# Streaming encoder layer on one core: value products carried past the ends of attention steps, softmax division moved to the output projection, and a new split of the exponentials' parts over ScalarE, VectorE and GpSimd

## The chip, the cores and the metric

The kernel runs on one core of one Trainium2 chip. The metric is the device time of one execution in microseconds (us); the time of a kernel is the median of its runs. Engine names are those of the profile: PE is TensorE's matmul side and PEld its weight loads, DVE is VectorE, ACT is ScalarE, POOL is GpSimd and SP is SyncE, which issues most DMAs.

## The reference

One layer of a hybrid encoder for two groups of requests: a prompt of 2048 new frames and a sample batch of 8 streams with 16 new frames each and 1024 cached ones. Channels are split: half go through a convolution module, half through attention with 8 heads of 64; both meet in one output projection, and a feed-forward network follows. All data are float32.

```
u, q, k, v, logf = _mixer_inputs(x, ...)          # rmsnorm, modulation, one input projection
# attention, per head, causal, with a cumulative forget bias
s = einsum('bqhd,bkhd->bhqk', q, k) * HEAD_DIM ** -0.5
s = s + (cum_q[..., :, None] - cum_k[..., None, :])
s = where(k_pos <= q_pos, s, NEG_INF)
attn = einsum('bhqk,bkhd->bqhd', softmax(s), v)
# convolution module: causal depthwise conv of width 31, LayerNorm over channels, silu
conv_out = silu(layernorm(conv(u_hist)))
mix = concat([conv_out, attn], -1) @ w_out
x = x + g1 * mix
h = rmsnorm(x) * (1 + sc2) + sh2
x = x + g2 * ((silu(h @ w_gate) * (h @ w_up)) @ w_down)
```

## The kernel before, in words

**Stages.** By the trace: the input projection of the convolution and value channels (0 to 345 us), the q and k projection with its norms (345 to 597), attention (597 to 1200), the output projection (1200 to 1407) and the feed-forward network (1407 to the end, line 1456 for its products). Large products are made of three matmuls in fp32r: an operand is split into a high part (a rounding copy) and a low part (what the copy lost), and high x high, high x low and low x high are summed. `parts_of` (L1158) makes the two parts: the copy on ACT (L1160), the subtraction on the engine that it is given (L1161).

**Prompt attention** runs in 16 steps, `STEPS`: head pair p = 0..3 by block of 512 queries qb = 0..3. A step has 8(qb+1) pieces, one for each tile of 128 keys and head; 320 in all. On the diagonal the pieces narrow from 512 to 384, 256 and 128 columns. For each piece `attend` (L954) issues two score matmuls (L973, L977; on the diagonal a mask, L979) into one of three banks `s`, an exponential on ACT (L981) into `ef` (three buffers), the high part of `e` on ACT (L1160), the low part (L1161) on GpSimd for every third piece and on VectorE otherwise, and, some pieces later, three value products (L964) into the bank `pv` of its head. Rows of `V` filled with ones make the sum of the exponentials in the other half of `pv`. `waiting` holds the pieces whose value products are still owed; it is local to a step, and at the step's end it is emptied. Then the step is normalized: four ACT copies of 64 rows (L998, L999), a logarithm and an exponential for the inverse sum (L1001, L1002), three DVE operations for one Newton step and the product (L1003 to L1005), and a store to `cat_d` (L1006).

**Maxima.** The exponentials need each query's maximum beforehand. `score_maxima` (L913) goes through the same scores transposed, 32 to 41 pieces ahead: one matmul (L934, on the diagonal L936 as well) into one of two banks `mx` and a DVE reduction (L937). At a step's end of its own the maxima are reduced to `Z` (L941), transposed by PE (L948, `pz`) and spread by two DVE products with the mask `bm` (L950) into eight rows of `Q2`, from which the score matmul subtracts them.

**Background.** `background` (L856) is woven in between: the LayerNorm of the convolution (`conv_norm`, L705, with the Newton steps of `newton_rsqrt` at L94 to L96) and the attention of the sample streams (`sample_setup`, `sample_batch`), whose products go into the bank `lane` (L716, L721, L1073, L1107). `last_parts` ends the preparation of the stage before, and `first_weights` loads and splits output weights during the last step.

**What sets the order.** Each engine runs its own list in order. The code is written as generators, and `weave` interleaves a step's parts in proportion to their length; a scheduler then orders each engine's list. `self.after` pins one instruction behind another: the first score of a piece stands behind a maximum 32 or more pieces ahead. K, Q1 and Q2 are loaded on GpSimd's queue (L889, L891, L903, L927); values (L906, `vraw`) and the rest on SP's. `vraw` shares a buffer (`rs`) with the logarithms of the step's end.

**Output projection.** `project_out` (L1178) takes 6 blocks of 360 or 368 columns. For each of 8 channel groups, the four of attention first, it loads `cr` from `cat_d` (L1196), for the convolution's applies silu (L1200), splits it into `ch` and `cl`, and accumulates 24 products into eight banks `acc` (L1144).

## Time and profile before

| | |
|---|---|
| time, median of 3 runs | 2820.78 us (2816.55 to 2822.61) |
| the profiled execution's own time | 2814.3 us |
| its span (first to last instruction) | 2812.5 us |
| mean granted PE clock | 0.98 |
| ACT busy in attention (597 to 1200 us) | 433.8 us |
| POOL busy in attention | 179.3 us |
| hardware DMA queue / software DMA queue | 570.73 MB / 25.42 MB |

How to read it: a group's row gives line, engine, operation, output and inputs, the count, the busy time, the mean duration of one in ns, and after the last bar the engine's idle time just before the group's instructions with what ended it. A row of the waits gives who waited for whom, the sum in us, how many times and the longest. PEclk is the granted clock of PE as a share of full speed. A busy time of PE holds waits that overlap: its instructions are pipelined and their records run into one another. Times of lines come from one profiled execution, which was 6.5 us shorter than the median.

### The profile page before, as it was taken

The numbers are of one execution on the slowest core, as the hardware profiler recorded it, in microseconds if no ns is written. First come the engines' busy times: TensorE is split into PE (matmuls) and PEld (weight loads), VectorE is DVE, ScalarE is ACT, GpSimd is POOL, SyncE is SP. The second block draws the span as 40 slices with busy tenths as digits, with TensorE's granted clock in tenths as the row PEclk, the third lists the DMA queues.
The fourth block names the chain that finished last, engine by engine and source line by source line (L and its number), as shares of the span: only waits on it lengthen the run. The fifth ranks groups of instructions, "written<-read, shape, count | busy, mean of one in ns | idle before, by whom it ended". The sixth has DMA issues, their size and how long they took to land. (4 is left out here: it accounts for less than half of the span.)

```text
span 2812.5 us, 48566 instructions
## 1 busy us (share of the span) xinstructions
PE 2718.6 (97%) x16536; PEld 2515.7 (89%) x16536; DVE 2161.9 (77%) x4235; ACT 1428.7 (51%) x2812; POOL 503.9 (18%) x685
## 2 busy tenths in 40 slices
PE   7999999999989999999999999999999999999999
PEld 6999988866667777698999989999999999999999
DVE  2798898989888787546397989877887778666765
ACT  4443323357776777744354446444554446555552
POOL 3454411243333222214201110000000000000000
PEclk9999999979999999999999999999999999999999
DMA  8753657673334766365576869866786769788883
GB/s 325 249 192 107 191 209 267 182 204 109 101 95 128 203 179 189 130 215 179 181 259 209 294 215 308 268 221 218 233 287 214 226 190 319 244 284 257 271 255 116
DMA packets 389960, 599.24 MB, mean 213 GB/s; under 512 B 47136, under 2 KB 250048, under 8 KB 387664
## 3 DMA queue, kind: packets, MB, share of 16 engines
q1 hardware_dynamic: 375248, 570.73, 62.8%
q0 software_dynamic: 14464, 25.42, 3.9%
q8 instruction: 130, 2.13, 0.3%
q14 instruction: 118, 0.97, 0.1%
HBM read 421.97 MB, written 174.08 MB: 212 GB/s over the span
## 5 line engine op out<-in xcount | busy, mean ns | idle before, releaser
L1456 PE MATMUL z<-rT,rW 128*128 128x360 f32 (+1 forms) x8316 | 1383.3, 328 | 5.5 <-ACT rW L1160 1.4
L1456 PEld LDWEIGHTS z<-rT,rW 128*128 128x128 f32 x8316 | 1378.7, 188 | 8.1 <-ACT rW L1160 2.4
L1160 ACT ACTIVATE rW<-rR 128x512 fp32r<-128x512 f32 x714 | 434.4, 617 | 386.8 <-PE z L1456 272.1
L1161 DVE TENSOR_TENSOR rW<-rR,rW 128x512 fp32r<-128x512 f32 x714 | 479.5, 676 | 154.5 <-ACT rW L1160 151.3
L700 DVE SCALAR_TENSOR_TENSOR cv<-cu,cpar,cv 128x384 f32<-128x384 f32 x580 | 311.6, 614 | 2.8 <-ACT cv L698 2.8
L964 PE MATMUL pv<-e,V 128*128 128x512 f32 (+3 forms) x960 | 268.9, 388 | 14.1 <-DVE e L1161 6.3
L964 PEld LDWEIGHTS pv<-e,V 128*128 128x128 f32 x960 | 167.9, 194 | 71.7 <-DVE e L1161 14.6
L937 DVE TENSOR_REDUCE M<-mx 128x1 f32<-128x512 f32 (+2 forms) x320 | 188.7, 603 | 50.2 <-PE mx L934 31.7
L981 ACT ACTIVATE ef<-s 128x512 f32<-128x512 f32 (+3 forms) x320 | 167.1, 532 | 116.7 <-PE s L979 47.1
L512 PE MATMUL z<-hqx,wqh 128*128 128x384 f32 (+1 forms) x768 | 196.6, 333 | 1.0 <-DVE logf L347 1.0
L1160 ACT ACTIVATE rT<-traw 128x360 fp32r<-128x360 f32 (+1 forms) x315 | 149.1, 501 | 91.7 <-DMA traw<-gt_d 62.9
L1161 DVE TENSOR_TENSOR rT<-traw,rT 128x360 fp32r<-128x360 f32 (+1 forms) x315 | 157.6, 531 | 45.0 <-ACT rT L1160 44.7
L1161 POOL TENSOR_TENSOR e<-ef,e 128x512 fp32r<-128x512 f32 (+3 forms) x106 | 127.2, 1200 | 347.4 <-ACT e L1160 180.7
L1160 ACT ACTIVATE e<-ef 128x512 fp32r<-128x512 f32 (+3 forms) x320 | 175.5, 567 | 4.0
L1161 DVE TENSOR_TENSOR e<-ef,e 128x512 fp32r<-128x512 f32 (+3 forms) x214 | 149.1, 704 | 35.4 <-ACT e L1160 34.4
L512 PEld LDWEIGHTS z<-hqx,wqh 128*128 128x128 f32 x768 | 135.7, 188 | 18.9 <-issue 15.3
L934 PE MATMUL mx<-K,Q 96*128 96x512 f32 (+2 forms) x320 | 134.3, 427 | 17.5 <-DVE M L937 11.3
L1144 PE MATMUL acc<-ch,woh 128*128 128x360 f32 (+1 forms) x384 | 127.4, 333 | 10.0 <-ACT ch L1160 4.6
L1384 DVE TENSOR_TENSOR rR<-rR 128x512 f32<-128x512 f32 (+1 forms) x136 | 93.4, 707 | 50.9 <-DMA rR<-w_down 44.1
L973 PE MATMUL s<-Q,K 128*128 128x512 f32 (+3 forms) x320 | 125.8, 393 | 3.4 <-ACT ef L981 3.4
L1144 PE MATMUL acc<-ch,wol 128*128 128x360 f32 (+1 forms) x384 | 126.9, 331 | 0.0
L512 PE MATMUL z<-hqx,wql 128*128 128x384 f32 (+1 forms) x384 | 126.4, 329 | 0.0
(306 smaller groups left out, 3935.4 us busy)
## 6 DMA issues: line engine op xcount, KB each, us to landing
rR<-sup_d SPq DMA_DIRECT2D x176, 256.0 KB
rR<-w_gate SPq DMA_DIRECT2D x132, 256.0 KB
traw<-gt_d SPq DMA_DIRECT2D x154, 180.0 KB
rR<-w_down SPq DMA_DIRECT2D x104, 256.0 KB
rR<-sdn_d SPq DMA_DIRECT2D x96, 256.0 KB
rR<-w_up SPq DMA_DIRECT2D x88, 256.0 KB
sup_d<-rR SPq DMA_DIRECT2D x88, 256.0 KB
wa<-w_ada SPq DMA_DIRECT2D x16, 1024.0 KB
```

What stands on the lines that cost most here:

```text
L512: nc.tensor.matmul(z[:, :n], w[:, m], x[:, :n], start=(c == 0 and k == 0), stop=(c == CB - 1 and k == 2))
L700: self.pin(nc.vector.scalar_tensor_tensor(dst, src, w, acc[i], ALU.mult, ALU.add))
L934: self.mx.append(nc.tensor.matmul(mx[:, :w], Q2[0:AUX, h, j * P:(j + 1) * P], K2[kb][0:AUX, h, :w], start=True, stop=not diag))
L937: nc.vector.tensor_reduce(M[:, i, kb:kb + 1], mx[:, :w], AX.X, ALU.max)
L964: nc.tensor.matmul(z[h][:, off:], V[kt // 4][:, v, kt % 4, h:h + 2, :].rearrange("p b c -> p (b c)"), e[:, x, off:], start=(kt == 0 and i ...
L973: first = nc.tensor.matmul(s[:, off:], K1[kb][:, h, sl], Q1[:, h, off:], start=True, stop=False)
L981: self.last_piece = nc.scalar.activation(ef[:, off:], s[:, off:], AF.Exp)
L1144: self.nc.tensor.matmul(z[:, :n], w[:, m], y, start=(first and i == 0 and k == 0), stop=(last and i == len(terms) - 1 and k == 2))
L1160: copy = self.nc.scalar.activation(hi, raw, AF.Copy)
L1161: engine.tensor_tensor(lo, raw, f32(hi), ALU.subtract)
L1384: nc.vector.tensor_tensor(t, x, y, op)
L1456: nc.tensor.matmul(z, W[:, x, m], t[:, y, :w], start=(k == 0 and i == 0), stop=(k == n - 1 and i == 2))
```

## The change

**Value products.** The list `waiting` belongs to the kernel and is emptied only behind the last step; a piece's value products follow five pieces behind its scores, those of another step among them. The first product of a piece is pinned behind the last score issued (`last_s`). A head's bank is taken when its first value product comes, and its end (`end_of_step`) comes with its last.

**End of a step and division.** `end_of_step` copies the head's whole bank to `zc` on ACT in one operation and stores the row of sums to `sum_d` and the undivided head to `cat_d`. `inverses`, woven into the next step (and behind the last one at once), loads the sums of both heads as 128 x 8, takes the reciprocal on DVE and stores it to `inv_d`. `project_out` loads two broadcast rows of `inv_d` for each attention operand and multiplies on DVE (24 multiplies, 48 loads).

**Parts of the exponentials.** For every second pair of pieces the high part is made by a copy on VectorE, for the others on ACT: 160 and 160. The low part of the first head goes to VectorE and of the second to GpSimd: 160 and 160, where before 214 and 106.

**Maxima.** One DVE copy of 8 rows and eight DMAs of one row each (128 columns) replace the products with `bm`; all maxima go into one row of `Q2`. The lead grows from 32 to at most 43 pieces.

**Queues.** K, Q1 and Q2 are loaded on SP's queue; `vraw` has a buffer of its own.

**Smaller edits.** One Newton step in place of two in the q/k norm and in `conv_norm`; `sample_setup` is cut by yields, and keys and biases of the sample streams are loaded a chunk or a stream ahead (`next_keys`, `next_bias`); background products are pinned behind the last score (`behind`); `xo` has 18 buffers in place of 20.

```diff
-            newton_rsqrt(nc, y, zp.tile([P, NB], F32, tag="t", name="rt", bufs=1)[:, :n], v, 2, self.pin)
+            newton_rsqrt(nc, y, zp.tile([P, NB], F32, tag="t", name="rt", bufs=1)[:, :n], v, 1, self.pin)
...
+            else:
+                parts.append((self.inverses(*STEPS[n - 1]), 4))
...
         drain(back)
+        drain(self.inverses(*STEPS[-1]))
...
-            nc.gpsimd.dma_start(K2[0:HD + 2], rows[HD:])
+            nc.sync.dma_start(f32(K2[0:HD + 2]), rows[HD:])
...
-        raw = self.awk.tile([P, 4, P], F32, tag="rs", name="vraw", bufs=1)
+        raw = self.awk.tile([P, 4, P], F32, tag="vr", name="vraw", bufs=1)
...
-        for h in range(2):
-            nc.vector.tensor_tensor(Q2[r, h, :].rearrange("r (j q) -> r j q", j=4),
-                                    pz[r, :].unsqueeze(1).broadcast_to([8, 4, P]),
-                                    self.bm[r, h, :].unsqueeze(2).broadcast_to([8, 4, P]), ALU.mult)
+        m = self.lp.tile([P, P], F32R, tag="mrow", name="mrow", bufs=1)
+        nc.vector.tensor_copy(m[r], pz[r])
+        for i in range(8):
+            nc.sync.dma_start(f32(Q2[AUX:AUX + 1, i // 4, i % 4 * P:(i % 4 + 1) * P]), f32(m[AUX + i:AUX + i + 1]))
...
         def value(kt, h, off, e):
+            if kt == 0:
+                z.append(self.bank("tr", "pv"))
...
+                if i == 0:
+                    self.after(product, self.last_s)
+            if kt == nkt - 1:
+                self.end_of_step(p, qb, h, z[h])
...
-                self.split3 = (self.split3 + 1) % 3
-                self.parts_of(e[:, 0, off:], e[:, 1, off:], ef[:, off:], nc.gpsimd if self.split3 == 0 else nc.vector)
-                waiting.append((kt, h, off, e))
-                if h and len(waiting) > len(self.eslots) - 3:
-                    value(*waiting.pop(0))
-                    value(*waiting.pop(0))
+                self.turn ^= h
+                if (h ^ self.turn) == 0:
+                    nc.vector.tensor_copy(e[:, 0, off:], ef[:, off:])
+                else:
+                    nc.scalar.activation(e[:, 0, off:], ef[:, off:], AF.Copy)
+                (nc.gpsimd if h else nc.vector).tensor_tensor(e[:, 1, off:], ef[:, off:], f32(e[:, 0, off:]), ALU.subtract)
+                self.waiting.append((value, kt, h, off, e))
+                while len(self.waiting) > min(len(self.eslots) - 2, 5):
+                    self.next_value()
                 yield
-        for w in waiting:
-            value(*w)
-
-        pvs, sm = (wk.tile([P, 512], F32, tag=k, name=k, bufs=1) for k in ("pvs", "sm"))
...
+        if n + 1 == len(STEPS):
+            while self.waiting:
+                self.next_value()
...
+    def end_of_step(self, p, qb, h, z):
+        if h == 0:
+            self.zc = self.awk.tile([P, 2, 512], F32, tag="zc", name="zc", bufs=1)
+        t = slice(qb * 512, qb * 512 + 512)
+        self.last_exp = self.nc.scalar.copy(self.zc[:, h], z)
+        o, x = slice(HD * h, HD * h + HD), HD - HD * h
+        self.nc.sync.dma_start(self.sum_d[2 * p + h:2 * p + h + 1, t], self.zc[x:x + 1, h])
+        self.last_store = self.nc.sync.dma_start(self.cat_d[o, 4 + p, t], self.zc[o, h])
...
+    def inverses(self, p, qb):
...
+        nc.sync.dma_start(r, self.sum_d[2 * p:2 * p + 2, t].rearrange("h (a c) -> a h c", c=4))
+        yield
+        nc.vector.reciprocal(r, r)
+        nc.sync.dma_start(self.inv_d[2 * p:2 * p + 2, t].rearrange("h (a c) -> a h c", c=4), r)
...
+                else:
+                    inv = cp.tile([P, NW], F32, tag="ci", name="ci", bufs=2)[:, :n]
+                    for h in range(2):
+                        load = nc.sync.dma_start(inv[HD * h:HD * h + HD], self.inv_d[2 * (c - 4) + h:2 * (c - 4) + h + 1, b0:b1].broadcast_to([HD, n]))
...
+                    nc.vector.tensor_tensor(raw, raw, inv, ALU.mult)
```

**What the order shows: the end of a step on PE.** PE's list of before at the end of the second step (`pv` are the step's value products, `s` scores, `mx` maxima, `lane` background):

```order
L973 MATMUL s_7578<-Q1_7147,K11_6652 128x128 [waits PE_49]
L977 MATMUL s_7578<-Q21_6650,K21_6648 128x128
L979 MATMUL s_7578<-masks_4132 128x128
L964 MATMUL pv_7360<-e_7554,V1_7012 128x256 [waits Activation_49]
L964 MATMUL pv_7360<-e_7554,V1_7012 128x256 [waits DVE_49]
L964 MATMUL pv_7360<-e_7554,V1_7012 128x256
L964 MATMUL pv_7359<-e_7572,V1_7012 128x128 [waits Activation_49]
L934 MATMUL mx_7408<-K23_6658,Q23_6667 128x384 [waits DVE_49]
L936 MATMUL mx_7408<-masks_4132 128x128
L716 MATMUL lane_7630<-cq_7671,ones_112 32x512 [waits Activation_49]
L964 MATMUL pv_7360<-e_7584,V1_7012 128x128 [waits Activation_49]
L716 MATMUL lane_7630<-cq_7674,ones_112 32x512 [waits Activation_49]
```
The rest of the value products stands in the next rows, and then the first score of the third step. PE's list of the changed kernel at the same place; there the score line is L984, the second score L988, the mask L990, the value product L971 and the maximum L939:

```order
L984 MATMUL s_7583<-Q1_7144,K11_6637 128x128 [waits Activation_49]
L988 MATMUL s_7583<-Q21_6635,K21_6633 128x128
L990 MATMUL s_7583<-masks_4134 128x128
L971 MATMUL pv_7401<-e_7542,V1_7013 128x256
L971 MATMUL pv_7401<-e_7542,V1_7013 128x256 [waits DVE_49]
L971 MATMUL pv_7401<-e_7542,V1_7013 128x256
L939 MATMUL mx_7421<-K20_6628,Q23_6652 128x512 [waits DVE_49]
L984 MATMUL s_7599<-Q1_7438,K10_6632 128x512 [waits DMAHW6_49,Activation_49]
L988 MATMUL s_7599<-Q22_6638,K20_6628 128x512 [waits DMAHW4_49,DMAHW5_49,DMAHW3_49,DMAHW2_49]
L971 MATMUL pv_7417<-e_7557,V1_7013 128x256
L971 MATMUL pv_7417<-e_7557,V1_7013 128x256 [waits Pool_49]
```
What moved: the third step's first score stands right behind the second step's last piece, and the value products still owed, three behind each score, follow it.

**The seam on SP.** SP's list of before where attention hands over to the output projection (`cr` are its operands, `raw` its weights, `pvs` the last step's result):

```order
L1323 DMA sp2_13363<-ident 128x128 [waits DVE_49,PE_49]
L1196 DMA cr_13385<-cat_d_71 128x368
L1196 DMA cr_13415<-cat_d_71 128x368
L1196 DMA cr_13445<-cat_d_71 128x368
L1196 DMA cr_13475<-cat_d_71 128x368
L1169 DMA raw_13507<-w_out 128x512 [waits PE_49]
L1169 DMA raw_13511<-w_out 128x512 [waits DMAHW3_49]
L1196 DMA cr_13515<-cat_d_71 128x368 [waits DMAHW6_49,DMAHW4_49,DVE_49]
L1169 DMA raw_13548<-w_out 128x512 [waits DMAHW5_49]
L1006 DMA cat_d_71<-pvs_13325 128x512 [waits DVE_49]
```
And of the changed kernel at the same place (L1023 and L1024 are the stores of `end_of_step`, L1033 and L1036 the load and the store of `inverses`, L1263 the operand, L1271 the inverses for it):

```order
L1023 DMA sum_d_80<-zc_13388 1x512 [waits Activation_49]
L1024 DMA cat_d_71<-zc_13388 64x512
L1023 DMA sum_d_80<-zc_13388 1x512 [waits Activation_49]
L1024 DMA cat_d_71<-zc_13388 64x512
L832 DMA cat_d_71<-catS_8605 128x128 [waits DMAHW5_49,DVE_49]
L1033 DMA inv_13398<-sum_d_80 128x2x4 [waits DMAHW6_49,DMAHW3_49,DMAHW1_49]
L832 DMA cat_d_71<-catS_8605 128x128 [waits DMAHW7_49]
L832 DMA cat_d_71<-catS_8605 128x128 [waits DMAHW0_49]
L832 DMA cat_d_71<-catS_8605 128x128
L1036 DMA inv_d_81<-inv_13398 128x2x4 [waits DMAHW2_49,DVE_49]
L1263 DMA cr_13449<-cat_d_71 128x368
L1271 DMA ci_13453<-inv_d_81 64x368 [waits DMAHW4_49,PE_49]
```
What moved: the operand loads, ahead of the last step's store before, now stand behind the last step's sums, inverses and their waits.

**A stretch of DVE** inside attention. Before (L937 reduces a maximum, L1161 makes a low part, L1003 to L1005 end a step, L950 spreads maxima):

```order
L937 TENSOR_REDUCE M_1_6670<-mx_12246 128x1 [waits PE_49]
L1161 TENSOR_TENSOR e_12360<-ef_12358,e_12360 128x512 [waits Activation_49]
L950 TENSOR_TENSOR Q22_6653<-pz_12250,bm_6633 8x512 [waits PE_49]
L950 TENSOR_TENSOR Q22_6653<-pz_12250,bm_6633 8x512
L937 TENSOR_REDUCE M_1_6670<-mx_12263 128x1 [waits PE_49]
L1083 RECIPROCAL rsx_10310<-rsx_10310 128x1 [waits Activation_49]
L1161 TENSOR_TENSOR e_12371<-ef_12369,e_12371 128x512 [waits Activation_49,Pool_49]
L937 TENSOR_REDUCE M_1_6670<-mx_12283 128x1 [waits PE_49]
L937 TENSOR_REDUCE M_1_6670<-mx_12295 128x1 [waits PE_49]
L1003 TENSOR_TENSOR sm_12330<-sm_12330,rs_12335 128x512 [waits Activation_49]
L937 TENSOR_REDUCE M_1_6670<-mx_12313 128x1 [waits PE_49]
L1004 SCALAR_TENSOR_TENSOR sm_12330<-sm_12330,rs_12335 128x512 [waits DVE_49]
```
And in the changed kernel (L942 reduces a maximum, L999 is the copy of a high part, L1002 the low part, L1228 splits values):

```order
L942 TENSOR_REDUCE M_0_6654<-mx_11920 128x1 [waits PE_49]
L1002 TENSOR_TENSOR e_12011<-ef_12009,e_12011 128x512 [waits Activation_49]
L1228 TENSOR_TENSOR V0_7012<-vraw_11877,V0_7012 128x4x2x64 [waits Activation_49]
L942 TENSOR_REDUCE M_0_6654<-mx_11951 128x1 [waits PE_49]
L942 TENSOR_REDUCE M_0_6654<-mx_11971 128x1 [waits PE_49]
L999 CAST e_12044<-ef_12042 128x512 [waits Activation_49]
L999 CAST e_12058<-ef_12056 128x512 [waits Activation_49,Pool_49]
L1002 TENSOR_TENSOR e_12044<-ef_12042,e_12044 128x512 [waits DVE_49]
L942 TENSOR_REDUCE M_0_6654<-mx_11985 128x1 [waits PE_49]
L942 TENSOR_REDUCE M_0_6654<-mx_12003 128x1 [waits PE_49]
L1002 TENSOR_TENSOR e_12072<-ef_12070,e_12072 128x512 [waits Activation_49]
```
What moved: the operations that end a step are gone, and of four pieces two high parts and two low parts stand on DVE.

More of the change, by code (lines that the diff above doesn't have):

```diff
@@ L715, in channel_mean @@
             for j in range(4):
-                nc.tensor.matmul(pm[32 * j:32 * j + 32, :n], self.ones[:, 0:32], src[j], start=True, stop=True,
+                self.behind(nc.tensor.matmul)(pm[32 * j:32 * j + 32, :n], self.ones[:, 0:32], src[j], start=True, stop=True,
                                  tile_position=(0, 32 * j))
@@ L782, in attention @@
         self.R.close()
-        self.split3 = 0
+        self.split3, self.turn, self.waiting, self.last_s = 0, 0, [], None
         self.Wout = {}
@@ L875, in background @@
         self.smc = self.after_attention.enter_context(self.pool(name="smc", bufs=2))
-        self.sample_setup(bank)
-        yield
+        yield from self.sample_setup(bank)
         for b in range(NS):
@@ L888, in keys @@
             rows = self.k_d[2 * p:2 * p + 2, :, t].rearrange("h r t -> r h t")
-            nc.gpsimd.dma_start(K2[0:HD + 2], rows[HD:])
+            nc.sync.dma_start(f32(K2[0:HD + 2]), rows[HD:])
             k1 = self.K1[(4 * p + kb) % 6]
-            nc.gpsimd.dma_start(k1, rows[0:P])
+            nc.sync.dma_start(f32(k1), rows[0:P])
             K1.append(k1)
@@ L926, in score_maxima @@
             t = slice(qb * 512, qb * 512 + 512)
-            nc.gpsimd.dma_start(Q2[0:HD], self.q_d[2 * p:2 * p + 2, 0:HD, t].rearrange("h r t -> r h t"))
+            nc.sync.dma_start(f32(Q2[0:HD]), self.q_d[2 * p:2 * p + 2, 0:HD, t].rearrange("h r t -> r h t"))
             for i in range(8):
@@ L957, in attend @@
         Q1, Q2 = self.Q1.pop(n), self.Q2[n % 4]
-        z = [self.bank("tr", "pv") for _ in range(2)]
         nkt = 4 * qb + 4
-        waiting = []
+        z = []
         def value(kt, h, off, e):
+            if kt == 0:
+                z.append(self.bank("tr", "pv"))
             for i, (v, x) in enumerate(((0, 0), (0, 1), (1, 0))):
-                nc.tensor.matmul(z[h][:, off:], V[kt // 4][:, v, kt % 4, h:h + 2, :].rearrange("p b c -> p (b c)"), e[:, x, off:],
-                                 start=(kt == 0 and i == 0), stop=(kt == nkt - 1 and i == 2))
+                product = nc.tensor.matmul(z[h][:, off:], V[kt // 4][:, v, kt % 4, h:h + 2, :].rearrange("p b c -> p (b c)"), e[:, x, off:],
+                                           start=(kt == 0 and i == 0), stop=(kt == nkt - 1 and i == 2))
+                if i == 0:
+                    self.after(product, self.last_s)
+            if kt == nkt - 1:
+                self.end_of_step(p, qb, h, z[h])
         for kt in range(nkt):
@@ L995, in attend @@
-        pvs, sm = (wk.tile([P, 512], F32, tag=k, name=k, bufs=1) for k in ("pvs", "sm"))
-        for h in range(2):
-            o, x = slice(HD * h, HD * h + HD), slice(HD - HD * h, P - HD * h)
-            nc.scalar.copy(sm[o], z[h][x])
-            nc.scalar.copy(pvs[o], z[h][o])
-        r = wk.tile([P, 512], F32, tag="rs", name="rs", bufs=1)
-        nc.scalar.activation(r, sm, AF.Ln)
-        self.last_exp = nc.scalar.activation(r, r, AF.Exp, scale=-1.0)
-        nc.vector.tensor_tensor(sm, sm, r, ALU.mult)
@@ L1004, in attend @@
-        nc.vector.scalar_tensor_tensor(sm, sm, 2.0, r, ALU.subtract, ALU.mult)
-        nc.vector.scalar_tensor_tensor(pvs, pvs, -1.0, sm, ALU.mult, ALU.mult)
-        self.last_store = nc.sync.dma_start(self.cat_d[:, 4 + p, qb * 512:(qb + 1) * 512], pvs)
+                self.turn ^= h
[3 more added lines that the diff above has]
+                    nc.scalar.activation(e[:, 0, off:], ef[:, off:], AF.Copy)
@@ L1008, in sample_setup, with behind, issue @@
+    def behind(self, op):
+        def issue(*args, **kw):
+            ins = op(*args, **kw)
+            self.after(ins, self.last_s)
+            return ins
+        return issue
     def sample_setup(self, bank):
@@ L1018, in sample_setup @@
         nc.gpsimd.memset(self.Qbd, 0.0)
+        self.kc, self.S = [], []
+        self.next_keys(0)
+        yield
+        yield
         for h in range(2):
@@ L1029, in sample_setup @@
         for kt in range(8):
-            nc.tensor.matmul(pt[:n, 2 * kt:2 * kt + 2], lf[:, kt, :], self.ones[:, 0:2], start=True, stop=True)
+            self.behind(nc.tensor.matmul)(pt[:n, 2 * kt:2 * kt + 2], lf[:, kt, :], self.ones[:, 0:2], start=True, stop=True)
         suf = sm.tile([P, 8], F32, name="suf")
@@ L1037, in sample_setup @@
             for i in range(4):
-                nc.tensor.matmul(pb[:n, i, :], lf[:, 4 * b + i, :], tri, start=True, stop=True)
+                self.behind(nc.tensor.matmul)(pb[:n, i, :], lf[:, 4 * b + i, :], tri, start=True, stop=True)
             nc.vector.tensor_tensor(
@@ L1072, in sample_batch @@
             for g in range(NP):
-                nc.tensor.matmul(pc[32 * g:32 * g + 32, :w], self.Qbd[:, g, b].rearrange("p h q -> p (h q)"), kt[:, g, :],
-                                 start=True, stop=True, tile_position=(0, 32 * g))
+                self.behind(nc.tensor.matmul)(pc[32 * g:32 * g + 32, :w], self.Qbd[:, g, b].rearrange("p h q -> p (h q)"), kt[:, g, :],
+                                              start=True, stop=True, tile_position=(0, 32 * g))
+            if c < 2:
+                self.next_keys(2 * b + c + 2)
+            else:
+                self.next_bias(b + 1)
             nc.vector.tensor_tensor(S[:, c0:c0 + w], S[:, c0:c0 + w], pc[:, :w], ALU.add)
@@ L1632, in host_layout @@
                             for w in range(2)], 1))
-    bm = np.zeros((P, 2, 4), np.float32)
-    for h in range(2):
-        for j in range(4):
-            bm[AUX + 4 * h + j, h, j] = 1
-    r["bm"] = bm
     r["sel"] = np.concatenate([
```

77 lines of the change are left out of this document (54 added, 23 removed).

## The prediction

> **What bounds the kernel now.** I read the page first (busy shares, then its costliest groups):
>
> ```profile
> span 2812.5 us, 48566 instructions
> ...
> PE 2718.6 (97%) x16536; PEld 2515.7 (89%) x16536; DVE 2161.9 (77%) x4235; ACT 1428.7 (51%) x2812; POOL 503.9 (18%) x685
> ...
> L1456 PE MATMUL z<-rT,rW 128*128 128x360 f32 (+1 forms) x8316 | 1383.3, 328 | 5.5 <-ACT rW L1160 1.4
> ```
>
> PE is the bound, but 97% is a mean over stages. The windows by stage come next (columns: us, then busy us of each engine with its instructions, granted clock, DMA share, GB/s):
>
> ```profile
> core 0: us, PE busy (x) PEld busy (x) DVE busy (x) ACT busy (x) POOL busy (x), PEclk, DMA share, GB/s
> ...
> 345.00:597.00 252.00, 250.69 (x1493) 210.31 (x1491) 233.13 (x573) 85.19 (x178) 59.60 (x101) 1.00 0.70 223
> ...
> 597.00:625.00 28.00, 23.30 (x52) 12.28 (x52) 23.75 (x46) 10.19 (x28) 10.30 (x12) 0.55 0.72 196
> 597.00:1200.00 603.00, 557.53 (x3177) 409.76 (x3176) 477.71 (x828) 433.80 (x879) 179.30 (x176) 0.95 0.51 145
> 1200.00:1407.00 207.00, 198.38 (x1183) 195.91 (x1184) 95.27 (x185) 83.34 (x160) 56.13 (x55) 0.99 0.59 193
> 1407.00:2812.00 1405.00, 1390.57 (x8383) 1386.76 (x8381) 1103.75 (x2139) 687.01 (x1342) 43.68 (x36) 0.99 0.76 244
> ```
>
> The feed-forward stage (1407 to 2812) and the q/k projection (345 to 597) have PE full; the change hardly touches them. Attention, 597 to 1200, holds the loss: 45.5 us of idle PE, and a granted clock of 0.95 that costs another 30 us (5% of 603). A busy PE also hides waits, since records overlap. The feed-forward stage gives the pace: 1405/8316 = 0.169 us for a product of 360 columns, 0.47 ns a column. Attention has 224 pieces of 512 columns and 32 each of 384, 256 and 128: 139,264 columns, in six products each (two scores, three values, one maximum), and some 250 masks of 128 columns: 868,000 columns, 407 us. Background products add about 65 (the largest two lines are below). So PE needs about 472 of 603 us; 30 go to the clock and about 100 to waits. Groups and waits of this window say on whom:
>
> ```profile
> L964 PE MATMUL pv<-e,V 128*128 128x512 f32 x672 | 210.4, 419 | 9.4 <-DVE e L1161 5.2 <-ACT e L1160 2.2 <-POOL e L1161 1.7
> ...
> L937 DVE TENSOR_REDUCE M<-mx 128x1 f32<-128x512 f32 x221 | 149.2, 684 | 37.4 <-PE mx L934 31.7 <-PE mx L936 4.6
> L1160 ACT ACTIVATE e<-ef 128x512 fp32r<-128x512 f32 x224 | 136.4, 632 | 2.0
> ...
> L1161 DVE TENSOR_TENSOR e<-ef,e 128x512 fp32r<-128x512 f32 x150 | 118.2, 795 | 25.2 <-ACT e L1160 24.7
> ...
> L1161 POOL TENSOR_TENSOR e<-ef,e 128x512 fp32r<-128x512 f32 x74 | 98.7, 1334 | 267.6 <-ACT e L1160 132.2 <-issue 40.3 <-PE pv L964 27.9
> ...
> L1073 PE MATMUL lane<-kc,Qbd 128*32 128x512 f32 x128 | 17.6, 622 | 4.1 <-DVE S L1075 4.1
> ...
> L1107 PE MATMUL lane<-vc,pT 128*32 128x128 f32 x512 | 16.0, 274 | 0.0
> ```
>
> ```profile
> PEld mx L934 <- DVE M L937: 27.1, 39, 1.8
> ...
> PEld pv L964 <- DVE e L1161: 14.6, 25, 1.3
> ```
>
> PE waits in turn for the maxima's reductions, which free its banks, and for the low parts: both on DVE, 79% busy here. Part of the idle time lies at ends of steps, where the value products are drained. The last end, in the timeline:
>
> ```profile
> 1193.90 0.27 PE L979 MATMUL s<-masks 128*128 128x128 f32 x1
> ...
> 1195.81 0.42 PE L964 MATMUL pv<-e,V 128*128 128x128 f32 x2
> ...
> 1197.03 0.86 PE L964 MATMUL pv<-e,V 128*128 128x128 f32 x3 [0.81 <-ACT e L1160]
> ```
>
> After the last score come the products still owed, then 0.8 us of nothing, then the rest.
>
> **The change part by part.** Changed line numbers are in the order above; durations below are of before.
>
> *Carried value products.* Only the last step drains. At the other 15 ends five scores of the next step now stand ahead of the step's last value products. I take 1.2 us each (the 0.8 shown and the short waits around it), 18 us; between 0.8 and 2, 12 to 30. The lost clock after 625 is about 17 us (30 less 0.45 × 28 = 12.6); half of it follows such gaps by my guess, 7 us.
>
> *High and low parts.* ACT gives up 160 of 320 copies, about 88 us, and is the bound nowhere in attention: nothing by itself. DVE takes 160 copies, 136 full pieces' worth. No copy of this shape from SBUF stands in the trace; the nearest is the subtraction below at 0.68 us alone, so at most 92 us, and I take 75 for a one-input operation. In return 54 of DVE's 214 low parts go to GpSimd, which then has 160 × 1.2 = 192 us in place of 127. What that does to DVE is seen here, DVE first, GpSimd second:
>
> ```profile
> 1019.81 0.68 DVE L1161 TENSOR_TENSOR e<-ef,e 128x512 fp32r<-128x512 f32 x1
> ...
> 1020.75 1.43 DVE L1161 TENSOR_TENSOR e<-ef,e 128x512 fp32r<-128x512 f32 x1
> ```
>
> ```profile
> 1020.09 1.55 POOL L1161 TENSOR_TENSOR e<-ef,e 128x512 fp32r<-128x512 f32 x1 [1.96 <-PE mx L934]
> ```
>
> A subtraction that starts under GpSimd's takes 1.43 us and ends with or after it; the group's mean of 795 against 680 is that.
>
> The Trainium skill ("VectorE: DVE Perf Modes", The perf-mode tier table) lets an fp32 copy in SBUF run at twice the rate of tensor_tensor (1227 against 2293 ns for 2048 elements). By that the copies would take about 0.36 us each, an estimate from its ratio and 49 us in all, and the sum would gain up to 26 us of DVE time over mine; no trace here shows it.
>
> *Ends of steps, spread, Newton.*
>
> ```profile
> L950 DVE TENSOR_TENSOR Q<-pz,bm 8x512 fp32r<-8x512 f32 x32 | 20.9, 692 | 0.7 <-PE pz L948 0.2
> ...
> L998 ACT COPY sm<-pv 64x512 f32<-64x512 f32 x32 | 18.6, 581 | 5.6 <-PE pv L964 4.9
> ...
> L1004 DVE SCALAR_TENSOR_TENSOR sm<-sm,rs 128x512 f32<-128x512 f32 x15 | 12.8, 850 | 0.0
> ...
> L1005 DVE SCALAR_TENSOR_TENSOR pvs<-pvs,sm 128x512 f32<-128x512 f32 x15 | 12.5, 832 | 0.0
> ...
> L1003 DVE TENSOR_TENSOR sm<-sm,rs 128x512 f32<-128x512 f32 x15 | 12.1, 806 | 0.0
> ...
> L94 DVE SCALAR_TENSOR_TENSOR ct<-cr 128x512 f32<-128x512 f32 x8 | 7.1, 886 | 0.0
> ```
>
> DVE loses 37 us of normalization, about 17 of the spread (a copy of 128 columns stays) and about 10 of Newton steps (half of this row and its two sisters). So DVE in attention: 478 − 38 (54 × 0.70) − 37 − 17 − 10 + 75 = 451, and the lock above grows with GpSimd's share from 21% to 33%: half as much again of its present 25 us or so, and the copies may meet it too, +15 to +50. I take 475, within 3 us of before: no gain from DVE's total, but it comes out of the ends of steps, where it stood in one block. I give 4 us for the bank of maxima that waited behind that block (of 27.1) and 3 for the lane's 4.1 (its loads and products now stand further apart). ACT frees a step's bank in one copy a head.
>
> *Queues.* K and Q loads move from GpSimd to SP, behind SP's stores of sums and rows, and 128 row transfers of 512 bytes follow. In before SP stands still for long:
>
> ```profile
> SPq L906 <- DVE sm L1004: 166.2, 12, 30.5
> ```
>
> That wait goes with the value rows' own buffer. The new SP waits are for the copies at ends of steps and for Q2's free buffer; behind them stand the next K loads, which are asked for seven or more pieces (about 12 us) early. I cost it at nothing; uncovered, one late load per step, 1 us × 15.
>
> *The start.* From 597 to 625 DVE is 85% busy and PE at half clock waits for the first maxima; a Newton step less in the q/k norm and direct transfers for the spread: −4 (0 to −8).
>
> *The seam.* Before, operands of the output projection are requested ahead of the last values; the first product follows the last value by 2.6 us:
>
> ```profile
> 1196.63 1.85 SPq L1196 DMA_DIRECT2D cr<-cat_d  x4
> ...
> 1200.49 0.67 PE L1144 MATMUL acc<-ch,woh 128*128 128x368 f32 x1 [2.60 <-ACT ch L1160]
> ```
>
> ```profile
> SPq L1298 <- DMA ht_d<-nx: 8.6, 8, 2.3
> ```
>
> Now they stand on SP behind the last step's inverses: copy 0.6, store of sums, load, reciprocal 0.2, store, load of inverses, then multiply 0.5 and high part 0.5. Four transfers at about 2.3 us with issue (the longest wait for a small one just quoted) make 9.2, the whole 11 to 12: +9 over before (+5 if transfers land in 1.3, +12 with a half-clock window behind the gap). No PE work stands there to cover it.
>
> *Output projection.* 24 multiplies and 48 transfers more; DVE is at 46% there, but each joins a chain that PE waits for at blocks' starts: +2 (0 to +6).
>
> Sum: −18 −7 −4 −3 −4 +9 +2 = −25; the loose pinning of background products and prefetched keys I put at −3 (0 to −10). −28: 2814.3 − 28 = 2786 for the profiled execution. That one is 6.5 us under the median of 2820.8, so the median is forecast at 2793. A difference of 0.2% (5.6 us) is what a measurement here can tell from none.
>
> **The rivals.** *PE at its pace.* If five pieces of lag cover most waits, attention loses 60 rather than 32 of its 130: total −60 − 4 + 9 + 2 = −53, 2768. For it: no drains, and a wait list made of many short waits (39 in 27.1 us). Against: DVE is not relieved.
>
> *VectorE bound through GpSimd.* Four full pieces now ask of DVE two copies (here at their upper 0.68), two low parts, four reductions: 8 × 0.68 = 5.4 us; PE has 24 products, 24 × 512 × 0.47 ns = 5.8. Two GpSimd subtractions of 1.3 us cover 40% of that time; each of four two-buffer operations meeting one for 0.65 us on average adds 1.0: 6.4, more than PE's 5.8. Over 68 such groups that is 41 us, which eats the 32 and leaves +9: with seam, projection and start +16, about 2837. It decides once copies too are held up by GpSimd. For it is this stretch, in which DVE is full and PE a fifth idle; against, before's reductions (from PSUM) keep 684 ns, and they are half of the load:
>
> ```profile
> 780.00:790.00 10.00, 8.00 (x43) 6.35 (x42) 9.91 (x21) 5.68 (x16) 4.05 (x4) 1.00 0.60 132
> ```
>
> The Trainium skill speaks for this rival: by "SBUF — State Buffer" (SBUF: two separate sides) a copy in a 2-port mode takes the shared port pair for the whole instruction just as a two-input operation does. The trace agrees for two inputs (1.43 against 0.68 us); for copies no run here shows it.
>
> *SP's queue.* The seam costs what I say, and inside attention loads queue late behind stores, 15 us of the 32 being lost: −28 + 15 = −13, at the worst about 0 if rows of the maxima also come late; 2808 to 2821.
>
> *It doesn't do what it says*: the order shows carried products and both splits; 2 in 100.
>
> **How the numbers follow.** Forecast 0.48, PE at its pace 0.22, VectorE bound 0.14, SP's queue 0.14, nothing 0.02. Faster: 0.48 + 0.22 + half of SP's = 0.77; same 0.09 (the rest of SP's and nothing); slower 0.14. The range starts at 2755 (PE at its pace with the seam at +5 and 10 more from the background) and ends at 2824, past SP's worst; it leaves out the VectorE case and a little below.
>
> **What would show it.** Right: value products after every score across ends of steps; PE idle in attention down from 45 to about 25 us; DVE's total near 475 in a stage of about 570; first output product 11 to 12 us after the last value. Wrong: low parts of DVE over 900 ns on average and copies over 0.7 (VectorE bound); K or Q2 awaited by PE (SP's queue); the seam under 5 us, or attention under 545 (PE at its pace).

## The result and the profile after

The changed kernel takes 2841.47 us (median of 4 runs, 2839.34 to 2847.12) against 2818.85 for the kernel before beside it: a ratio of 1.0084, 95% interval 1.0066 to 1.0102. It is slower by 0.84%, outside the range and against the sign of the forecast. The profiled execution took 2839.3 us, with a span of 2837.5.

Where the time went is read from the first and last start of three lines, from the views of the score line, the value line and the products of the output projection (count, then ns as least/median/most, then first to last start in us). Before:

```profile
L973 PE MATMUL s<-Q,K x320: 221/395/796, 624.6 to 1193.6; 128*128 128x512 f32 x112, 128*128 128x384 f32 x16, 128*128 128x256 f32 x16, 128*128 128x128 f32 x16
```

```profile
L964 PE MATMUL pv<-e,V x960: 220/393/796, 631.3 to 1197.6; 128*128 128x512 f32 x138, 128*128 128x256 f32 x25, 128*128 128x384 f32 x15, 128*128 128x128 f32 x14
```

```profile
L1144 PE MATMUL acc<-ch,woh x384: 321/329/674, 1200.5 to 1406.7; 128*128 128x360 f32 x128, 128*128 128x368 f32 x64
...
L1144 PE MATMUL acc<-cl,woh x384: 321/327/412, 1204.8 to 1407.0; 128*128 128x360 f32 x128, 128*128 128x368 f32 x64
```

After:

```profile
L984 PE MATMUL s<-Q,K x320: 222/396/735, 619.0 to 1182.1; 128*128 128x512 f32 x112, 128*128 128x384 f32 x16, 128*128 128x256 f32 x16, 128*128 128x128 f32 x16
```

```profile
L971 PE MATMUL pv<-e,V x960: 219/392/735, 624.1 to 1187.3; 128*128 128x512 f32 x139, 128*128 128x256 f32 x20, 128*128 128x384 f32 x17, 128*128 128x128 f32 x16
```

```profile
L1211 PE MATMUL acc<-ch,woh x384: 322/330/673, 1200.8 to 1432.8; 128*128 128x360 f32 x128, 128*128 128x368 f32 x64
...
L1211 PE MATMUL acc<-cl,woh x384: 321/327/502, 1205.1 to 1433.2; 128*128 128x360 f32 x128, 128*128 128x368 f32 x64
```

| us | before | after | difference | forecast |
|---|---|---|---|---|
| up to the first score | 624.6 | 619.0 | −5.6 | −4 |
| attention: first score to last value product | 573.0 | 568.3 | −4.7 | −35 |
| seam: to the first output product | 2.9 | 13.5 | +10.6 | +9 |
| output projection: first to last product | 206.5 | 232.4 | +25.9 | +2 |
| the rest | 1405.5 | 1404.3 | −1.2 | 0 |

The differences sum to the 25.0 us between the spans. Two terms failed: attention, which gave a seventh of its gain, and the output projection. (The −35 joins the terms of drains, clock, bank, lane and background.)

The windows by stage of the changed kernel, for attention and for the fourth block of the output projection (from its first product to the first of the fifth):

```profile
597.00:1200.00 603.00, 548.16 (x3164) 412.70 (x3164) 455.29 (x866) 323.49 (x643) 200.40 (x174) 0.94 0.50 144
```

```profile
1310.70:1365.40 54.70, 40.38 (x210) 37.64 (x209) 28.68 (x58) 18.51 (x36) 16.02 (x15) 0.87 0.65 202
```

and the same block before:

```profile
1304.40:1341.40 37.00, 34.62 (x208) 33.19 (x209) 24.95 (x48) 14.15 (x27) 16.11 (x15) 1.00 0.69 223
```

DVE has less work in attention than before (455 against 478 us), so more work on it is not what ate the gain, and ACT has 110 us less. This one block of the projection takes 17.7 us more, 54.7 against 37.0, with PE idle for 14.3 and the granted clock at 0.87; the second, third and fifth are 2 to 3 us longer each. Waits in attention of the changed kernel:

```profile
PEld mx L939 <- DVE M L942: 45.4, 50, 3.2
...
PE mx L939 <- DVE M L942: 25.8, 22, 3.0
...
DVE inv L1035 <- DMA inv<-sum_d: 20.9, 9, 4.6
```

PE's waits for value products have gone, as meant; those for the maxima's banks rose (PEld 27.1 to 45.4, PE 11.3 to 25.8). And there is a new line: DVE, which works its list in order, stands nine times, 20.9 us in all, until the sums of a step have come back from memory, since `inverses` put a reciprocal into its list. Everything behind it in DVE's list waits, and the reductions that free the maxima's banks are among it. The forecast costed this load only at the seam.

The seam in the timeline, from the copy of the last step to the first output product:

```profile
1187.19 1.07 ACT L1021 COPY zc<-pv 128x512 f32<-128x512 f32 x2 [0.71 <-PE pv L971]
...
1188.59 0.44 SPq L1023 DMA_DIRECT2D sum_d<-zc  x1
...
1190.36 0.39 SPq L1033 DMA_DIRECT2D inv<-sum_d  x1
...
1192.27 0.20 DVE L1035 RECIPROCAL inv<-inv 128x8 f32<-128x8 f32 x1 [4.07 <-DMA inv<-sum_d]
1192.50 0.37 SPq L1036 DMA_DIRECT2D inv_d<-inv  x1
1192.91 0.47 SPq L1263 DMA_DIRECT2D cr<-cat_d  x1
1193.48 1.11 SPq L1271 DMA_DIRECT2D ci<-inv_d  x2
...
1199.66 0.54 DVE L1274 TENSOR_TENSOR cr<-cr,ci 128x368 f32<-128x368 f32 x1 [7.19 <-DMA ci<-inv_d]
...
1200.80 0.67 PE L1211 MATMUL acc<-ch,woh 128*128 128x368 f32 x1 [13.10 <-ACT ch L1227]
```

This is the chain of the prediction, step by step, but not with its prices. From the store of the sums to the reciprocal it took 3.7 us where two transfers of 2.3 were allowed; the last hop, from the store of the inverses to the multiply, took 7.2 where two more were. And most of that hop is the operand's own load, which now is asked for late. The run e1 below has neither the loads of the inverses nor the multiply, and there the operand still takes 5.1 us from its request to the copy on ACT:

```profile
1194.41 1.89 SPq L1263 DMA_DIRECT2D cr<-cat_d  x4
...
1199.53 0.51 ACT L1227 ACTIVATE ch<-cr 128x368 fp32r<-128x368 f32 x1 [8.40 <-DMA cr<-cat_d]
```

Its seam is 11.3 us, so the loads of inverses and the multiply make only 2.2 of the 13.5.

### The profile page after: what moved, and what is told of

Read it like the earlier page. It is cut to its first block, busy times and chain, and to the rows that moved or that the text cites. A ratio compares the mean times of both kernels' runs of the same rounds, so it can differ in the third digit from the quotient of the medians.

```text
span 2837.5 us, 48644 instructions
## 1 busy us (share of the span) xinstructions
PE 2719.1 (96%) x16536; PEld 2525.4 (89%) x16536; DVE 2142.7 (76%) x4284; ACT 1323.1 (47%) x2588; POOL 529.3 (19%) x675
## 5 line engine op out<-in xcount | busy, mean ns | idle before, releaser
L1228 DVE TENSOR_TENSOR rW<-rR,rW 128x512 fp32r<-128x512 f32 x714 | 479.9, 677 | 163.9 <-ACT rW L1227 159.1
L971 PE MATMUL pv<-e,V 128*128 128x512 f32 (+2 forms) x960 | 259.1, 380 | 0.0
L1002 POOL TENSOR_TENSOR e<-ef,e 128x512 fp32r<-128x512 f32 (+3 forms) x160 | 187.9, 1176 | 360.6 <-DVE e L999 151.6
L942 DVE TENSOR_REDUCE M<-mx 128x1 f32<-128x512 f32 (+2 forms) x320 | 190.9, 604 | 51.7 <-PE mx L939 35.6
L971 PEld LDWEIGHTS pv<-e,V 128*128 128x128 f32 x960 | 171.2, 195 | 30.0 <-issue 1.2
L1228 DVE TENSOR_TENSOR rT<-traw,rT 128x360 fp32r<-128x360 f32 (+1 forms) x315 | 158.7, 534 | 31.0 <-ACT rT L1227 30.6
L939 PE MATMUL mx<-K,Q 96*128 96x512 f32 (+2 forms) x320 | 138.0, 438 | 27.4 <-DVE M L942 25.8
L939 PEld LDWEIGHTS mx<-K,Q 96*128 96x128 f32 x320 | 64.2, 201 | 74.7 <-DVE M L942 45.4
L984 PE MATMUL s<-Q,K 128*128 128x512 f32 (+3 forms) x320 | 127.7, 399 | 0.1
L1211 PE MATMUL acc<-cl,woh 128*128 128x360 f32 (+1 forms) x384 | 125.6, 337 | 0.4 <-DVE cl L1228 0.4
```

The source lines that it names most:

```text
L939: self.mx.append(nc.tensor.matmul(mx[:, :w], Q2[0:AUX, h, j * P:(j + 1) * P], K2[kb][0:AUX, h, :w], start=True, stop=not diag))
L942: nc.vector.tensor_reduce(M[:, i, kb:kb + 1], mx[:, :w], AX.X, ALU.max)
L971: product = nc.tensor.matmul(z[h][:, off:], V[kt // 4][:, v, kt % 4, h:h + 2, :].rearrange("p b c -> p (b c)"), e[:, x, off:], start=(kt = ...
L984: first = nc.tensor.matmul(s[:, off:], K1[kb][:, h, sl], Q1[:, h, off:], start=True, stop=False)
L1002: (nc.gpsimd if h else nc.vector).tensor_tensor(e[:, 1, off:], ef[:, off:], f32(e[:, 0, off:]), ALU.subtract)
L1211: self.nc.tensor.matmul(z[:, :n], w[:, m], y, start=(first and i == 0 and k == 0), stop=(last and i == len(terms) - 1 and k == 2))
```

## The experiments

Ratios are to the kernel before on the same chip, with 95% intervals; the stages come from each run's profile as in the table above. Three of these kernels (the changed one, e1, e2) differ by no edit in attention and took 568.3, 568.8 and 574.7 us there: a difference in attention under 6 us between single profiles says nothing, and there the ratios decide. The projection scatters as well: the changed kernel and the five that share its projection (e3, e6, e7, e11, e12) took 232 to 238 us there, three without the division (e1, e8, e10) 215 to 224, those with 20 buffers and the division at the ends of steps 205 to 208. Attention, seam and projection are in us.

| run | ratio (interval) | attention | seam | projection |
|---|---|---|---|---|
| changed | 1.0084 (1.0066 to 1.0102) | 568.3 | 13.5 | 232.4 |
| e1 | 1.0041 (1.0026 to 1.0055) | 568.8 | 11.3 | 218.6 |
| e2 | 1.0031 (1.0018 to 1.0044) | 574.7 | 11.7 | 220.4 |
| e3 | 1.0101 (1.0079 to 1.0122) | 574.6 | 13.3 | 234.7 |
| e4 | 1.0042 (1.0026 to 1.0059) | 575.1 | 2.9 | 218.7 |
| e5 | 0.9950 (0.9929 to 0.9970) | 563.6 | 6.4 | 208.3 |
| e6 | 1.0053 (1.0036 to 1.0071) | 556.9 | 12.7 | 236.1 |
| e7 | 1.0160 (1.0138 to 1.0182) | 593.8 | 12.2 | 236.7 |
| e8 | 0.9934 (0.9909 to 0.9958) | 551.3 | 3.0 | 215.4 |
| e9 | 0.9911 (0.9896 to 0.9927) | 559.8 | 2.9 | 207.0 |
| e10 | 0.9955 (0.9942 to 0.9968) | 556.5 | 2.8 | 223.5 |
| e11 | 1.0037 (1.0023 to 1.0052) | 551.3 | 12.9 | 236.4 |
| e12 | 1.0058 (1.0042 to 1.0074) | 560.4 | 13.2 | 237.9 |
| e13 | 0.9955 (0.9940 to 0.9970) | 564.4 | 4.8 | 207.2 |
| e14 | 1.0003 (0.9991 to 1.0014) | 571.4 | 3.4 | 206.6 |
| e15 | 0.9948 (0.9931 to 0.9965) | 568.7 | 5.0 | 205.4 |
| e16 | 0.9909 (0.9879 to 0.9939) | 557.5 | 4.7 | 205.9 |
| e17 | 0.9875 (0.9843 to 0.9907) | 550.5 | 3.0 | 208.0 |

**The output projection: e1, e2, e4.** In e2 the tile of ones is filled once, ahead of the blocks, by GpSimd.

```diff
-                    inv = cp.tile([P, NW], F32, tag="ci", name="ci", bufs=2)[:, :n]
...
-                    nc.vector.tensor_tensor(raw, raw, inv, ALU.mult)
+                    pass
```

> The changed kernel without the division in the output projection: no loads of the inverses there, no multiply (its attention output stays undivided; all else, the inverses too, is as in the changed kernel). Theory D (the loss of 26 us in the output projection is the division's doing): the projection falls from 232 us back to about 207, the first output product comes about 9 us after the last value instead of 13.5, and the time falls by about 30 us, to some 2811 us. Rival X (the two buffers taken from xo): the projection stays above 225 us and the time above 2830. Rival V (VectorE in attention is the loss): attention is untouched, so the time stays at 2841 within 4 us.

```diff
-                    nc.vector.tensor_tensor(raw, raw, inv, ALU.mult)
+                    nc.vector.tensor_tensor(raw, raw, one[:, :n], ALU.mult)
```

> As the run without the division, but the 24 multiplies stay, by a tile of ones that is already there: the 48 loads of inverses alone are left out (the output stays undivided). If the loads on SP's queue and their landing are what the division costs: as the run without the division, within 4 us. If it is the multiply in VectorE's row: 10 us or more above it, near the changed kernel.

```diff
-                x = sp.tile([P, NW], F32, tag="x", name="xo", bufs=20)
+                x = sp.tile([P, NW], F32, tag="x", name="xo", bufs=18)
```

> The kernel before with 18 buffers for xo in place of 20 and nothing else. Rival X (the buffers): the output projection grows by 10 us or more, 2829 us or above. Theory D: no change from the kernel before, 2819 within 4 us.

Neither theory alone was right; each has half. Without the division the projection falls by 14 us and stays 12 above the kernel before; with 18 buffers in the kernel before it rises by those 12 (206.5 to 218.7). The 24 multiplies without their loads cost nothing that shows (220.4 against 218.6), though DVE stands in front of them for 34.0 us until `cr` lands. So 12 to 14 us come with the 48 loads; whether by their time on SP's queue or by DVE's further wait for them (13.8 us in 7 waits in the changed kernel) was not tried. The buffers act in one block, the fourth, 51.2 us in e4 against 37.0:

```profile
1301.90:1353.10 51.20, 39.64 (x209) 37.77 (x209) 23.75 (x49) 15.30 (x29) 16.01 (x15) 0.86 0.60 196
...
1322.00:1332.00 10.00, 7.47 (x26) 7.24 (x27) 6.05 (x17) 4.27 (x9) 5.42 (x5) 0.50 0.26 90
```

```profile
SPq L1211 <- DMA x_d<-xo: 5.9, 7, 1.7
```

Loads of `xT` wait on SP until a store has freed their buffer (5.9 us, 2.1 with 20 buffers); DVE, which adds a bank's product to `xT` and so frees the bank, waits for them (8.5 us against 3.2), and PE waits for the bank (9.7 against 4.3). For some 10 us of this block the granted clock is 0.50. The buffers' total is shown by e4; the chain, and that the clock falls because PE idles, are read from the trace and have no run of their own.

**The inverses in attention: e3, e8, e10.** e3 put three more yields between the load and the reciprocal.

> The changed kernel with the reciprocal of a step's sums three yields further behind the load that it waits for. Theory R (in attention VectorE stands still for the landing of the sums, 25 us in 10 waits, and the maxima's reductions behind it hold PE): VectorE's wait for the sums falls below 5 us, attention gets 5 to 12 us shorter, 2830 to 2836 us in all. Rival V (VectorE is bound by its work and by GpSimd): the wait goes and the time stays within 3 us of 2841.

It tested nothing: in the order that was run, the reciprocal stands as close behind its load as in the changed kernel, and DVE still waited as long.

```profile
DVE inv L1038 <- DMA inv<-sum_d: 21.6, 9, 5.5
```

e8 leaves the inverses out of the kernel without division, e10 only the reciprocal:

```diff
-                parts.append((self.inverses(*STEPS[n - 1]), 4))
...
-        drain(self.inverses(*STEPS[-1]))
```

> As the run without the division, and without the inverses too: no loads of sums, no reciprocals, no stores of them (the attention output stays undivided). Theory R (VectorE's 21 us of waits for the sums to land cost PE 5 to 12 us in attention): attention falls from some 569 to 562 us or less. Theory M: within 4 us. In both the seam falls from 11 to about 5 us, since no inverse stands ahead of the operands on SP.

```diff
-        nc.vector.reciprocal(r, r)
```

> The run without the division, with the inverses' loads and stores left in and only the reciprocal on VectorE left out (what is stored are the sums; the attention output stays undivided). Theory R (it is VectorE that stands behind the load): attention as without any inverses, 551 us within 4, against 569 with the reciprocal. Theory Q (SP's queue: its waits for the copies and the sums delay what stands behind them): attention near 569 us. The seam, where SP no longer waits for VectorE but still for two landings, falls from 11 to about 7 us in both.

Theory R holds in the main. Without the reciprocal attention falls from 568.8 to 556.5 us (551 within 4 was expected), without all of the inverses to 551.3. By the ratios e10 is 0.86% or 24 us below e1, of which the seam is 8.5. The waits for the maxima's banks fall, from 47.0 and 27.3 us in e1 to these in e10:

```profile
PEld mx L939 <- DVE M L942: 34.3, 41, 3.6
PE mx L939 <- DVE M L942: 18.0, 18, 3.2
```

So sixteen operations of 0.2 us cost some 12 us in attention by where they stand, by a single profile of each and with the scatter above. (In e10 the first operand load moved ahead of the inverses in SP's list, so its seam of 2.8 us is not a test of the landings; that of e8, 3.0 us, shows the chain to be the seam's whole cost.)

**The split: e6, e11, e12, e13.** e6 takes all of the new split back, e11 the copies, e12 the low parts, each in the changed kernel; e13 is e5 (below) with e11's edit:

```diff
-                if (h ^ self.turn) == 0:
-                    nc.vector.tensor_copy(e[:, 0, off:], ef[:, off:])
-                else:
-                    nc.scalar.activation(e[:, 0, off:], ef[:, off:], AF.Copy)
+                nc.scalar.activation(e[:, 0, off:], ef[:, off:], AF.Copy)
```

> The changed kernel with the high parts all on ScalarE and every third low part on GpSimd, as before. Theory V (the new split binds VectorE and GpSimd, and so eats what the carried products gain): attention, 568 us in the changed kernel, falls below 560. Rival S (the split pays, by relief of ScalarE): attention grows beyond 575. Theory M (neither; PE's waits for the maxima set the pace): within 4 us of 568.

> The changed kernel with all high parts copied on ScalarE, the low parts still half on GpSimd. If the copies' work in VectorE's row is what the new split costs: attention falls from 568 to about 557 us as with the whole split undone, and the time by about 11 us. If it is GpSimd's longer hold of the shared port by 160 low parts: attention stays within 4 us of 568.

> The changed kernel with half of the high parts copied on VectorE, but every third low part on GpSimd as before. If GpSimd's longer hold is what the new split costs: attention falls to about 560 us. If it is VectorE's work: attention grows beyond 572 us, since VectorE has 54 low parts more (33 us of work).

> The kernel with the division at the ends of steps (20 buffers for xo) with all high parts copied on ScalarE and half of the low parts on GpSimd. If the copies on VectorE are what the new split costs and GpSimd's larger share helps: attention below 556 us, and the time at or below that of the run with the whole old split, 0.9% and more under the kernel before. If GpSimd's share costs too: near the run with the whole new split, 0.5% under.

The new split costs: with all of it undone the ratio falls by 0.31% in the changed kernel (e6), by 0.39% in e5 (to e9): 9 and 11 us. Which half costs stays open. In the changed kernel undoing the copies alone gives 0.47% and the low parts alone 0.26%, together more than the whole; on e5 the copies alone give nothing (e13, 0.9955 against 0.9950), and what remains between e13 and e9 is GpSimd's larger share. The sum of VectorE's work is not it: e12 has more of it than the changed kernel (469 against 455 us from 597 to 1190) and is faster.

**Carried products: e7, e14, e15.** e7 empties the list at each step's end in the changed kernel, e15 in e9; e14 carries the products in the kernel before and changes nothing else.

```diff
-        if n + 1 == len(STEPS):
-            while self.waiting:
-                self.next_value()
+        while self.waiting:
+            self.next_value()
```

> The changed kernel with the waiting products emptied at the end of each step, as before. The forecast's term (18 us, 25 with the clock): attention grows from 568 to 586 or more. Theory M: it grows by less than 6 us, since what PE waits for at the ends are the maxima and not the products.

> The kernel before with the carried value products alone (five pieces of lag, the first product pinned behind the last score, the bank taken with the first product); division, split, queues and maxima as before. The forecast's term: 18 to 25 us less in attention, 2790 to 2797 us. Rival (the carried products need ScalarE's copies, the queues and the other edits to pay): within 6 us of the kernel before.

> The kernel of e9 (0.9% faster than before) with the waiting products emptied at each step's end. If the gain of e9 needs the carrying: the kernel is no faster than before, 2810 us or above, attention 575 or longer. If the gain is the other edits': within 5 us of e9, 2790 us.

The value of carrying depends on its company: 0.76% or 21 us in the changed kernel, 0.37% or 10 us in e9, none in the kernel before, all by the ratios. (Of e9's 0.89% the other 0.52% is there without carrying, in e15; no run takes the edits behind it apart.) What took the place of the waits in e14:

```profile
PEld mx L934 <- DVE M L937: 42.0, 57, 4.1
...
PE mx L934 <- DVE Q L950: 11.5, 9, 3.2
```

The waits for value products are gone (PE's for DVE's low parts fell from 6.3 to 1.0 us), and those for the maxima took their place: the banks (27.1 to 42.0) and the spread into `Q2` (3.1 to 11.5). That these ate the gain is not shown: e17, the fastest kernel below, waits as long for its banks (42.9 us in PEld, 19.5 in PE, against 42.0 and 15.9 in e14). Why carrying alone gains nothing stays open.

**The versions that beat both: e5, e9, e16, e17.** e5 puts the division back to the ends of steps and xo back to 20 buffers, and `vraw` shares its buffer with the logarithms again; e9 is e5 with the split as before; e16 and e17 take out of e9 the new spread of the maxima and the loads on SP (one of the four loads is shown):

```diff
-            nc.sync.dma_start(f32(k1), rows[0:P])
+            nc.gpsimd.dma_start(k1, rows[0:P])
```

> The changed kernel with the division taken back to the ends of steps as in the kernel before (four copies of 64 rows, logarithm, exponential, three VectorE operations), the products still carried, no inverses and none in the output projection, and 20 buffers for xo again. Theory D+X (division in the projection and the two buffers are the whole loss): the projection is back at 207 us and the seam at about 3, which gives back 36 us of the changed kernel's time; attention pays up to 10 us for 38 us of VectorE work. So 10 us faster than the kernel before, at the least no slower. Rival (carried products gain nothing): within 4 us of the kernel before.

> The kernel with the division at the ends of steps (20 buffers for xo), and the high and low parts split as before as well: what stays of the change is the carried products, the queues, the row transfers of the maxima and the small edits. If the parts add up as in the runs before (the new split costs attention 11 us): some 11 us faster than with the division at the ends alone, 1% below the kernel before, attention near 552 us. If the split only costs together with the inverses' waits: within 4 us of the division at the ends alone.

> The kernel of e9 with the maxima spread as before, by two VectorE products with the mask and no row transfers. If carried products pay only once the maxima's spread is off VectorE (in e14 PE waits 11.5 us for it, in the kernel before 0.6): 8 us or more slower than e9, attention near 568. If not: within 5 us of e9.

> The kernel of e9 with K, Q1 and Q2 loaded on GpSimd's queue as before. If the queues carry the gain (GpSimd's 37 us of issue, its waits for PE in front of low parts): 6 us or more slower than e9. If not: within 5 us.

The times of e5 and e9 came as expected (14 us below the kernel before, and 11 more), though e9's attention took 559.8 us and not 552. The spread is worth nothing that shows (e16), so the wait for `Q2` in e14 isn't by itself what ate the gain. e17 met neither of its two cases: it is faster than e9, by 0.36% or some 10 us in the ratios. The intervals overlap a little, so this gain is at the edge of what the runs can tell. SP in e9 stands before the value rows for their shared buffer, and before a Q load for PE to free its buffer, and with it all that is queued behind:

```profile
SPq L908 <- DVE sm L1023: 70.2, 9, 23.8
...
SPq L905 <- PE s L987: 42.5, 8, 11.9
```

In e17 that second line is gone from SP; that it is the cause was not tried by itself, and PE in e9 stands for a load of Q only once, 3.5 us. e17 (carried products, one Newton step, the sample streams' loads ahead, the rows of the maxima, all else as before) is the fastest, 1.25% below the kernel before, with attention at 550.5 us.

## Why the prediction was wrong, point by point

- **Carried products, 18 + 7 us.** The drains were real, and in the changed kernel undoing the carrying costs 21 us by the ratios, near the term. What failed is that it was added as a gain over the kernel before, as if nothing took the place of these waits: alone it gives 0 there (e14). The prediction asked of DVE's total work only, found it unchanged, and did not price the next wait, the maxima's banks, though it had quoted that wait's row. That wait grew (27.1 to 42.0 us in e14); that it is what ate the gain is not shown.
- **The ends of steps on VectorE, −4 and −3.** The prediction counted what the division no longer does and left out what its successor adds there: the reciprocal was priced at 0.2 us and at the seam alone. In attention DVE stands 21 us in front of it, and taking it out gives back some 12 us (e1 against e10). This is the first step that failed, an added wait without the question of what is queued behind it.
- **The parts, nothing.** The copies took 78 us in all where 75 were assumed (a median of 0.42 us, but a mean of 0.52 at 512 columns). DVE's work fell to 455 us where 475 was forecast, since its low parts did not grow longer (799 ns on average at 512 columns against 795). Still the new split costs 9 to 11 us (e6, e9). The rival that VectorE is bound gave 2837 us, close to the 2841 measured, but that is luck: it had attention 9 us longer, and attention got shorter; copies over 0.7 us and low parts over 900 ns, its signs, did not come.
- **The queues, nothing.** Open. e17 gains some 10 us over e9, at the edge of the noise, in kernels whose value rows hold up SP longer for their shared buffer (70.2 us in e9, 39.5 for their own in the changed kernel). In the changed kernel no K or Q load stands among PE's waits, which was the prediction's own sign for this.
- **The seam, +9.** Right in place, 10.6 measured, and gone without the inverses (e8). The size is in part luck: the prediction did not price the operand's own late load, 5.1 us in e1, and the hop it gave to the inverses' load and the multiply adds only 2.2.
- **The output projection, +2.** The second step that failed. The multiplies are free (e2), but their 48 loads cost 12 to 14 us, and the two buffers given up cost 12 (e4); the prediction gives the buffers no price at all.
- **The start, −4.** −5.6 measured; no run took its edits apart.

Start from e17, 1.25% or 35 us below the kernel before, and add the parts so found: split 9 to 11, inverses in attention 12 to 17, seam 8 to 10, loads 12 to 14, buffers 12. That makes +18 to +29, against +24 by the changed kernel's ratio; with the 10 us between e9 and e17 it would be +28 to +39. The parts overlap, and single profiles carry some 6 us of scatter.

## What to carry to other kernels

A result that makes a round trip through memory cost almost nothing here where it was computed (0.2 us), and a lot where an engine that works in order stood for the landing: price each added wait by what is queued behind it, for DVE as for SP. When a wait is removed, look at the wait ranked next in the same window before booking the gain. And a buffer count in a diff is a timing edit: undo it alone, as e4 did, before blaming the code beside it.

## What the runs showed of the hardware

The copy of a high part on VectorE, its view by line in the changed kernel:

```profile
L999 DVE CAST e<-ef x160: 252/419/1298, 621.5 to 1183.9; 128x512 fp32r<-128x512 f32 x128, 128x256 fp32r<-128x256 f32 x32
```

The median of 0.42 us for mostly 512 columns stands against 0.68 for a subtraction of that size, somewhat above an estimate of 0.36 by the ratio of 1227 to 2293 ns in the Trainium skill ("VectorE: DVE Perf Modes", The perf-mode tier table). The longest, 1.30 us, is three times the median. What stretches a copy is seen beside GpSimd's subtractions:

```profile
962.29 0.41 DVE L999 CAST e<-ef 128x512 fp32r<-128x512 f32 x1
...
965.30 1.28 POOL L1002 TENSOR_TENSOR e<-ef,e 128x512 fp32r<-128x512 f32 x1 [1.24 <-issue]
965.69 1.18 DVE L999 CAST e<-ef 128x512 fp32r<-128x512 f32 x1
```

The second copy starts under a subtraction of GpSimd and ends 0.29 us after it. Of the copies of 512 columns that the trace shows singly, the 90 with no such subtraction beside them took 0.37 to 0.43 us, and the 26 that started under one took 0.85 in the median, up to 1.30. The Trainium skill ("SBUF — State Buffer", SBUF: two separate sides) says that a copy in a 2-port mode is kept out while GpSimd holds the shared port; the trace agrees. So copies are held up, as the rival had it, but only about one in five, and their mean stays at 0.52 us.
